# A hybrid encoder layer on one core: rows normed before the split, ten tile pairs by seven quarter products, linear attention in one written order

## The chip, the core and the metric

The kernel runs on one core of a Trainium2 chip. [...] Work moves between engines through semaphores. The metric is the time of one execution on the device in microseconds (us). The kernel of before takes 1973.33 us, the median of three runs (1972.96 to 1973.87).

## What is computed

One layer of a streaming encoder on two request groups, 1024 prompt tokens and 32 sample tokens, side by side as T = 1056 columns. D = 1024 features lie as 8 row tiles of 128 partitions.

```
h = rms(x);  z = h @ w_in  -> q,k,v,r,gate-rank | band q,k,v | gates gA,gB
A: linear attention, 4 heads: S = exp(b_last) S + (k exp(b_last - b))^T v,
   o = scores v + (q exp(b)) S,   b = cumsum(log sigmoid(...)) / 16,
   scores with a decay for each channel;  rms per head, * silu(r)
B: softmax attention over the own and the 8 last 64-token chunks, 8 heads
x += rms((sigmoid(gA) * (A @ w_a) + sigmoid(gB) * (B @ w_b)) @ w_out)
x += rms(conv feed-forward);   x += rms(sigmoid(rms(x) @ w_g) * (p @ w_ple))
```

The input product has 52 output tiles of 128 columns of w_in: 4 q, 4 k, 8 v, 8 r, 12 of the band, 8 gA and 8 gB, and a narrow one of 16 columns for the gate rank.

## The kernel before

All large products are split in two halves to keep float32 accuracy: a tensor x becomes xh (rounded to the matmul format) and xl = x - xh, a weight becomes whi and wlo, and one product takes three matmuls: whi.xh, whi.xl, wlo.xh (`product`, L224 to L230). The columns are cut into three chunks of 352 (`CHUNKS`). A tile of the input product is 8 row tiles x 3 matmuls x 3 chunks = 72 matmuls.

Up to L373 stands the start. The side input p is multiplied with w_ple first (L302 to L312), while the eight rows of x arrive. The rows are split with the norm's gain but without the norm itself (L320, L321); their squares are added on ACT, POOL and DVE (L324 to L330), and the norm's inverse root is made afterwards (L342). It is applied when a tile leaves PSUM: `to_tile` (L352) multiplies by `rstd` on DVE. `project(n, evac)` loads a weight tile (`weights`, L198; ACT makes the high half in L207, DVE or POOL the low one in L208), does its 72 matmuls and evicts each chunk.

Band attention (from L386) goes over four head pairs. Each projects q, k and v (`band_project`), splits them and turns v, and then does nine pieces of work for each of the two heads (`band_head`: scores, exponentials, transposes, product with v). After each pair `gates(n)` projects some of the 16 gate tiles, takes their sigmoid (L547) and stores them in DRAM (`BAND_GATES` = 1, 1, 1, 0).

The linear attention goes over four heads (last loop before `xp.release()`): `gla_project` makes q, k, v and turns v (L644); `gla_rest` makes r and its silu (L654); `gla_head` makes the decay b (matmul L674, Exp and Ln L677 and L678, nine scans L681), and then goes through four segments of 256 tokens (the last with 32 sample tokens more). A segment has for each of six levels a difference (L698), two exponentials (L699, L700) and two factors (L701, L702); then for each 128-token block seven small products (L730, L731), eight masked copies into `scores` (L733, L736), the output (L744, L746), a transposed key (L750), and the state's update (L755, L760). The output's norm and the product with silu(r) end it (L770 to L779). `gates` projects 2, 3, 2 and 6 gate tiles after the heads (`GLA_GATES`), and `weight_sum` lets POOL issue sums of weight blocks that the down product uses far later.

Branch B's product (L812 to L833) loads the band's results and their softmax sums (`d_ob`, `d_inv`), multiplies and splits them into `bh` and `bl`, which lie where xh lay; branch A's product, the output product, the feed-forward's up and down products and the last gate follow.

What sets the order: up to the branch products nothing is written out. The framework's scheduler gives each engine a list by program order as priority, and moves ready work ahead of work that must wait. `tc.high_priority()` raises weight splits and evictions. From the output product on, `tc.manual_schedule` keeps PE, DVE and ACT in program order. There the up product is already computed by block sums and seven quarter products in place of eight (L1188 to L1279). SP and POOL issue their transfers in their own order. Large row buffers come from the pool `ev`, tag "ev", with `EVB` = 5 buffers: each `evt()` takes the next one and waits until its last reader is done. PSUM has 3 banks of tag "mm" for projections, 3 of "one" and one double bank "two" (`PS_BAND`).

Of the kernel before, what the change touches and what calls it, by code (L numbers as in the profile page):

```python
# [11 lines left out]
F32 = mybir.dt.float32  # L12
# [35 lines left out]
EVB = 5  # L48
# [6 lines left out]
GLA_GATES = (2, 3, 2, 6)  # L55
# [33 lines left out]
ORD0 = 'rvvqk'  # L89
# [23 lines left out]
def emit(tc, a):  # L113
# [18 lines left out]
    banks = list(PS_BAND)  # L132
# [142 lines left out]

    d_pl = tl(dram, [8, P, T], tag="d_pl")
    xp = pool("xp", side="right")
    pp = pool("pp", side="right")
    ph = tl(pp, [P, 2, T], F32R, tag="ph")
    pl = tl(pp, [P, 2, T], F32R, tag="pl")  # L280
    pin = [tl(pp, [P, T], tag="pin", bufs=2) for kt in range(2)]
    for i in range(WARM):
        pe.matmul(ps_mm()[:, :P], onesM, onesM, start=True, stop=True)
    for kt in range(2):
        ac.dma_start(pin[kt][:, chunk(0)], a["p"][kt, :, chunk(0)])
    wple = [weights(a["w_ple"][0], ve, 4)]
    for c in range(NC):
        s = chunk(c)
        for kt in range(2):
            if c:  # L290
                dma.dma_start(pin[kt][:, s], a["p"][kt, :, s])
            split_hi_lo(ph[:, kt, s], pl[:, kt, s], pin[kt][:, s])
    dma.dma_start(vec, a["vec"])
    st = pool("st", side="right")
    xin = [tl(st, [P, T], tag="xin", bufs=XB) for kt in range(KT)]
    for kt in range(KT):
        if kt == XFIRST:
            wple.append(weights(a["w_ple"][1]))
        dma.dma_start(xin[kt], a["x"][kt])
    dma.dma_start(convst, a["state_conv"])  # L300
    for n in range(KT):
        hi, lo = wple[n // 4]  # L302
        z = evt()
        for c in range(NC):
            s = chunk(c)
            ps = ps_mm()[:, : s.stop - s.start]
            product(ps, hi, lo, [(2 * (n % 4) + k, k) for k in range(2)], lambda k: ph[:, k, s], lambda k: pl[:, k, s])
            if c in PLE_DVE:
                ve.tensor_copy(z[:, s], ps)
            else:  # L310
                ac.activation(z[:, s], ps, AF.Copy)
        dma.dma_start(d_pl[n], z)  # L312


    xh = tl(xp, [P, KT, T], F32R, tag="xh")
    xl = tl(xp, [P, KT, T], F32R, tag="xl")
    accx = tl(st, [P, T], tag="accx")
    for kt in range(KT):
        x = xin[kt]
        ac.activation(xh[:, kt], x, AF.Copy, scale=col(G_PRE_MIX + kt))  # L320
        ve.scalar_tensor_tensor(xl[:, kt], x, col(G_PRE_MIX + kt), xh[:, kt], op0=ALU.mult, op1=ALU.subtract)  # L321
        q = accx if kt == 0 else x
        if kt % 2:
            po.tensor_tensor(q, x, x, op=ALU.mult)  # L324
        else:
            ac.activation(q, x, AF.Square)
        if kt == 1:
            ve.scalar_tensor_tensor(accx, x, 8 * EPS, accx, op0=ALU.add, op1=ALU.add)
        elif kt > 1:
            ve.tensor_tensor(accx, accx, x, op=ALU.add)  # L330
    import contextlib
    def hpri(f):
        return tc.high_priority() if f else contextlib.nullcontext()

    log_exp()
    for c in range(NC):
        s = chunk(c)
        inv_rms(rstd(s), accx[:, s], "D", st, split=NS_START)
    st.release()
    pp.release()  # L340

# [9 lines left out]
    def to_tile(t):  # L351
        return lambda ps, s: ve.tensor_tensor(t[:, s], ps, rstd(s), op=ALU.mult)  # L352


    ap = pool("ap")
    d_alr = tl(dram, [80, T], F32R, tag="d_alr")
    alr = evt()[:16]
    war = tl(ap, [P, KT, 16], tag="war")
    dma.dma_start(war, a["w_alr"])
    was = tl(ap, [P, KT, 48], F32R, tag="was")  # L360
    ve.tensor_copy(was[:, :, 0:16], war)
    ve.tensor_copy(was[:, :, 16:32], war)
    ve.tensor_tensor(was[:, :, 32:48], war, was[:, :, 0:16], op=ALU.subtract)
    for c in range(NC):
        s = chunk(c)
        ps = ps_mm()[:48, : s.stop - s.start]
        for kt in range(KT):
            pe.matmul(ps, was[:, kt], xh[:, kt, s], start=(kt == 0), stop=False)
            pe.matmul(ps, was[:, kt], xl[:, kt, s], start=False, stop=(kt == KT - 1))
        ac.activation(alr[:, s], ps[32:48], AF.Copy)  # L370
        ve.tensor_tensor(alr[:, s], ps[0:16], alr[:, s], op=ALU.add)
        ve.tensor_tensor(alr[:, s], alr[:, s], rstd(s, 16), op=ALU.mult)
    ast = tl(ev, [P, T], F32R, tag="ev", bufs=EVB)[:80]  # L373
    po.memset(ast.bitcast(F32), 0.0)
    ac.activation(ast[0:16], alr, AF.Copy)
    ve.tensor_tensor(ast[32:48], alr, ast[0:16], op=ALU.subtract)
    ac.activation(ast[64:80], alr, AF.Copy)
    po.dma_start(d_alr, ast)

    ap.release()  # L380
# [5 lines left out]
    def band_project(hp):  # L386
# [4 lines left out]
        project(QB0 + hp, lambda ps, s: ve.scalar_tensor_tensor(qf[:, s], ps, 0.125, rstd(s), op0=ALU.mult, op1=ALU.mult))  # L391
        project(KB0 + hp, to_tile(kf))
        project(VB0 + hp, to_tile(vf))
# [145 lines left out]
    d_ga = tl(dram, [8, P, T], tag="d_ga")  # L539
    d_gb = tl(dram, [8, P, T], tag="d_gb")  # L540
    todo_gates = [(n, w, d) for n in range(8) for w, d in ((GA0, d_ga), (GB0, d_gb))]

    def gates(cnt):
        for n, w0, dst in todo_gates[:cnt]:
            g = evt()
            project(w0 + n, to_tile(g))
            ac.activation(g, g, AF.Sigmoid)  # L547
            dma.dma_start(dst[n], g)
        del todo_gates[:cnt]

    d_inv = tl(dram, [4, 2, 9 * P], tag="d_inv")
    for hp in range(4):
# [29 lines left out]
        gates(BAND_GATES[hp])  # L582
# [6 lines left out]
    d_sr = tl(dram, [8, P, T], tag="d_sr")  # L589
    gp = pool("gp")  # L590
    wa2 = None

    masks, eye, scores, scores_s = None, None, [], None


    def constants():
        nonlocal masks, eye, scores_s
        masks = tl(gp, [P, 7, 64], U8, tag="masks")
        mf = tl(gp, [P, 64], tag="mf", bufs=2)
        for l in range(7):  # L600
            m = 1 << l
            mf = tl(gp, [P, 64], tag="mf", bufs=2)
            po.memset(mf, 1.0)
            v = mf.rearrange("p (n m) -> p n m", m=m)
            pat = [[-2 * m, 64 // m], [0, m]]
            po.affine_select(out=v, in_=v, pattern=pat, compare_op=ALU.is_ge, fill=0.0, base=0, channel_multiplier=1)
            pat = [[2 * m, 64 // m], [0, m]]
            po.affine_select(out=v, in_=v, pattern=pat, compare_op=ALU.is_ge, fill=0.0, base=m - 1, channel_multiplier=-1)
            ve.tensor_copy(masks[:, l], mf)
        eye = tl(gp, [P, P], U8, tag="eye")  # L610
        ve.tensor_copy(eye, ident)
        for i in range(2):
            scores.append(tl(gp, [P, P], tag=f"scores{i}"))
            po.memset(scores[i], 0.0)
        scores_s = tl(gp, [NS, NS], tag="scores_s")
        po.memset(scores_s, 0.0)
# [1372 lines left out]
```

## Time and profile before

| | us |
|---|---|
| median of three runs | 1973.33 |
| profiled execution, span from first to last instruction | 1970.8 |
| from the first product of x's tiles (gate rank) to the first product of branch B | 39.72 to 904.11 |
| PE busy | 1924.6 |
| DVE busy | 1251.5 |
| ACT busy | 951.2 |
| POOL busy | 405.4 |

The program has one core, and PE's granted clock is 0.994 of full speed on average. A line of the groups view gives: the line of the kernel, engine and operation, the tile written and the tiles read, the shape, the count; then busy time in us, the mean of one in ns; then the engine's idle time just before these instructions and what ended it. A line of the timeline begins with the start and the duration in us. A line of the windows view gives a stretch and its length, for each engine the busy us and the number of instructions, then PE's clock, the share of the 16 DMA engines in use and GB/s. A line of the transfers view gives the destination and source, queue, count, size and the median time from issue to landing.

### The profile page before, as it was taken

How to read it: one execution, taken by the hardware profiler on the slowest of the kernel's cores; microseconds unless marked ns; L12 is line 12 of the kernel's file. 1: busy time of each engine (PE TensorE's matmuls, PEld its weight loads, DVE VectorE, ACT ScalarE, POOL GpSimd, SP SyncE). 2: the span in 40 equal slices, each digit the busy share in tenths (PEclk: the TensorE clock that was granted, in tenths of full speed). 3: DMA queues.
4: the chain of work that ended last, by engine and by line, in shares of the span. 5: the costliest groups of instructions: out<-in, count | busy, mean ns of one | idle time of the engine just before them, and what ended most of it. 6: DMA issues, size and time to landing. Idle time of an engine off the chain costs nothing.

```text
span 1970.8 us, 34508 instructions
## 1 busy us (share of the span) xinstructions
PE 1924.6 (98%) x13594; PEld 1886.2 (96%) x13594; DVE 1251.5 (64%) x2546; ACT 951.2 (48%) x1747; POOL 405.4 (21%) x470
## 2 busy tenths in 40 slices
PE   8999999999999999998999999999999999999996
PEld 7999999999999999998999989999999999999996
DVE  7556556457366475466554576787777766557776
ACT  6456455455364463564323454443333344555545
POOL 4322322143112131121120111111121211000112
PEclk9999999999999999999999999999999999999998
DMA  7212121166226253227744345644345459887755
GB/s 283 69 57 75 59 70 57 51 185 180 82 89 172 81 155 88 97 77 240 267 163 133 103 136 194 213 137 137 109 121 114 113 141 310 276 290 233 246 158 105
DMA packets 107005, 289.04 MB, mean 147 GB/s; under 512 B 11668, under 2 KB 34012, under 8 KB 106204
## 3 DMA queue, kind: packets, MB, share of 16 engines
q1 hardware_dynamic: 78924, 198.45, 31.1%
q0 software_dynamic: 27632, 88.04, 16.5%
q8 instruction: 106, 1.74, 0.4%
q14 instruction: 55, 0.45, 0.1%
q10 hardware_dynamic: 288, 0.36, 0.1%
HBM read 198.49 MB, written 111.39 MB: 157 GB/s over the span
## 4 chain that ended last, share of the span: by engine, by line
PE 80%; DVE 10%; ACT 4%; DMA 3%; issue 2%; SPq 0%; DVEq 0%; ACTq 0%
PE mm L228 13%; PE mm L229 13%; PE mm L230 13%; PE two L1212 6%; PE two L1214 6%; PE two L1213 6%; PE two L1665 3%; PE two L1664 3%; PE two L1663 3%; PE one L508 2%; PE two L730 2%; PE one L466 1%; DVE d L698 1%; PE two L450 1%; PE one L744 1%
## 5 line engine op out<-in xcount | busy, mean ns | idle before, releaser
L228 PE MATMUL mm<-xh,whi 128*128 128x352 f32 x1248 | 412.1, 330 | 0.0
L230 PE MATMUL mm<-xh,wlo 128*128 128x352 f32 x1248 | 411.9, 330 | 0.0
L229 PE MATMUL mm<-xl,whi 128*128 128x352 f32 x1248 | 409.7, 328 | 0.0
L208 POOL TENSOR_TENSOR wlo<-raw,whi 128x512 fp32r<-128x512 f32 x130 | 183.8, 1422 | 680.6 <-ACT whi L207 628.1
L228 PEld LDWEIGHTS mm<-xh,whi 128*128 128x128 f32 x1248 | 235.3, 189 | 1.6 <-DVE ev L352 0.4
L229 PEld LDWEIGHTS mm<-xl,whi 128*128 128x128 f32 x1248 | 235.0, 188 | 1.7 <-issue 0.3
L230 PEld LDWEIGHTS mm<-xh,wlo 128*128 128x128 f32 x1248 | 234.6, 188 | 1.1
L1665 PE MATMUL two<-d,wlo 128*128 128x264 f32 x616 | 175.5, 285 | 1.2 <-DVE wlo L1407 1.2
L1664 PE MATMUL two<-d,whi 128*128 128x264 f32 x616 | 174.7, 284 | 2.0 <-DVE d L1358 2.0
L1663 PE MATMUL two<-d,whi 128*128 128x264 f32 x616 | 174.7, 284 | 0.4 <-ACT d L1357 0.4
L207 ACT ACTIVATE whi<-raw 128x512 fp32r<-128x512 f32 (+1 forms) x146 | 89.4, 621 | 156.8 <-PE mm L229 95.3
L1214 PE MATMUL two<-mh,wlo 128*128 128x264 f32 x576 | 163.0, 284 | 0.0
L1213 PE MATMUL two<-ml,whi 128*128 128x264 f32 x576 | 162.9, 284 | 0.0
L1212 PE MATMUL two<-mh,whi 128*128 128x264 f32 x576 | 161.2, 284 | 0.0
L1664 PEld LDWEIGHTS two<-d,whi 128*128 128x128 f32 x616 | 115.8, 188 | 2.4 <-DVE d L1358 2.4
L1665 PEld LDWEIGHTS two<-d,wlo 128*128 128x128 f32 x616 | 115.6, 188 | 1.6 <-DVE wlo L1407 1.6
L1663 PEld LDWEIGHTS two<-d,whi 128*128 128x128 f32 x616 | 116.4, 189 | 0.6 <-ACT d L1357 0.6
L1214 PEld LDWEIGHTS two<-mh,wlo 128*128 128x128 f32 x576 | 108.4, 188 | 0.0
L1213 PEld LDWEIGHTS two<-ml,whi 128*128 128x128 f32 x576 | 108.4, 188 | 0.0
L1212 PEld LDWEIGHTS two<-mh,whi 128*128 128x128 f32 x576 | 107.3, 188 | 0.0
L352 DVE TENSOR_TENSOR ev<-mm,rstd 128x352 f32<-128x352 f32 x120 | 61.4, 518 | 54.5 <-PE mm L230 53.9
L1202 ACT ACTIVATE whi<-ws 128x512 fp32r<-128x512 f32 x72 | 45.4, 631 | 102.0 <-PE two L1213 76.7
(534 smaller groups left out, 5178.6 us busy)
## 6 DMA issues: line engine op xcount, KB each, us to landing
raw<-in_w_in SPq DMA_DIRECT2D x52, 512.0 KB, 4.0
uraw<-d_b SPq DMA_DIRECT2D x34, 528.0 KB, 5.7
d_b<-av POOLq DMA_DIRECT2D x33, 528.0 KB, 3.5
d_ws<-in_w_down POOLq DMA_DIRECT2D x24, 704.0 KB, 12.1
raw<-in_w_up SPq DMA_DIRECT2D x27, 512.0 KB, 3.7
wraw<-d_ws SPq DMA_DIRECT2D x16, 704.0 KB, 6.0
d_b<-gc POOLq DMA_DIRECT2D x11, 792.0 KB, 5.7
sraw<-in_w_up SPq DMA_DIRECT2D x17, 512.0 KB, 4.6
```

The costliest lines, as they stand in the source:

```text
L207: ac.activation(hi[-1][:, d], raw[:, b], AF.Copy)
L208: eng.tensor_tensor(lo[-1][:, d], raw[:, b], hi[-1][:, d], op=ALU.subtract)
L228: pe.matmul(ps, h, xh(kt), start=(first and i == 0), stop=False)
L229: pe.matmul(ps, h, xl(kt), start=False, stop=False)
L230: pe.matmul(ps, l, xh(kt), start=False, stop=(last and i == n - 1))
L352: return lambda ps, s: ve.tensor_tensor(t[:, s], ps, rstd(s), op=ALU.mult)
L1212: pe.matmul(ps[:, j, :HC], w[0][:, k], x[0][:, k, s], start=st, stop=False, skip_group_check=True)
L1213: pe.matmul(ps[:, j, :HC], w[0][:, k], x[1][:, k, s], start=False, stop=False, skip_group_check=True)
L1214: pe.matmul(ps[:, j, :HC], w[1][:, k], x[0][:, k, s], start=False, stop=sp_, skip_group_check=True)
L1663: pe.matmul(o, wh, xh_[:, s], start=(k == 0 and p in (0, 4, 5)), stop=False, skip_group_check=True)
L1664: pe.matmul(o, wh, xl_[:, s], start=False, stop=False, skip_group_check=True)
L1665: pe.matmul(o, wl, xh_[:, s], start=False, stop=(k == HD - 1 and p in (3, 4, 6)), skip_group_check=True)
```

## The change

1. The start (up to the first tile pairs) is written out in one fixed order for PE, DVE and ACT. x is loaded by column halves; each half's norm is made between the products of p, the rows are multiplied with gain and norm, and only then split. Evictions no longer multiply by the norm, and most go to ACT. The band's first q, k and v tiles and the gate rank are computed by halves of 528 columns (two matmuls of 264) and stored; the band loads them back. Beside the second half, DVE makes the block sums of x for the next step.

2. The eight r tiles, the eight gB tiles and the first four gA tiles are computed as ten pairs by `in_strassen`: two weight tiles and x form a 2 x 2 block product, done with seven quarter products of 4 row tiles x 2 x 264 columns x 3 matmuls = 168 matmuls a pair. This stage comes before band attention. The order in it is the scheduler's.

3. Between band pair 2 and 3 the tiles k and q of head 0 are projected and stored. No gate tile is left in the band's stage.

4. The linear attention is in one written order over 16 segments. Decay differences, exponentials and factors are made for the segment after the one whose products run; masked copies and state updates take two blocks at once; the root and result of a segment come in the next one. Three projection chunks ("units") stand in each segment: 12 tiles of heads 1 to 3 and the last four gA tiles, whose sigmoid is moved to branch A's product.

5. `EVB` goes from 5 to 4.

```diff
-EVB = 5
+EVB = 4
-GLA_GATES = (2, 3, 2, 6)
+GLA_GATES = (0, 0, 1, 3)
+GA_DENSE = 4
...
+    def x_norm(h, i):
+        for k in range(2 * i, 2 * i + 2):
+            ve.scalar_tensor_tensor(xrow(k)[:, h], xrow(k)[:, h], col(G_PRE_MIX + k), ys[h.start], op0=ALU.mult, op1=ALU.mult)
+        ac.activation(xh[:, 2 * i : 2 * i + 2, h], xrow(2 * i, 2)[:, :, h], AF.Copy)
+
+    def x_low(h, i):
+        b = slice(2 * i, 2 * i + 2)
+        ve.tensor_tensor(xl[:, b, h], xrow(2 * i, 2)[:, :, h], xh[:, b, h], op=ALU.subtract)
...
+    S = {0: [lambda: p_split(1)], 1: [lambda: p_split(2)], 2: [lambda: first_load(0)],
+         4: [lambda: x_square(one, 0)], 5: [lambda: x_square(one, 1)],
+         6: [lambda: x_add(one, 1)], 7: [lambda: x_square(one, 2), lambda: wple.append(next(raw_split(raws[1], eng=po))), lambda: first_load(1)], 8: [lambda: x_add(one, 2)],
+         9: [lambda: x_square(one, 3)], 10: [lambda: x_add(one, 3), lambda: x_sums(one)],
+         12: [lambda: x_inverse(one)], 13: [lambda: x_norm(one, 0)], 14: [alr_weights, lambda: first_split(2), lambda: first_load(2)],
...
+    plain_half(0, one, first_hook)
+    plain_half(1, one, second_hook)
+    plain_half(2, one)
+    alr_half(one)
...
+    plain_half(0, two, sum_hook(0))
+    plain_half(1, two, sum_hook(1))
+    plain_half(2, two, sum_hook(2))
+    alr_half(two)
...
+        def mul(ps, w, n, first, last):
+            x = XIN[n]
+            for j in range(2):
+                s = slice(j * HC, (j + 1) * HC)
+                for k in range(HK):
+                    st, sp_ = first and k == 0, last and k == HK - 1
+                    pe.matmul(ps[:, j, :HC], w[0][:, k], x[0](k, s), start=st, stop=False, skip_group_check=True)
+                    pe.matmul(ps[:, j, :HC], w[0][:, k], x[1](k, s), start=False, stop=False, skip_group_check=True)
+                    pe.matmul(ps[:, j, :HC], w[1][:, k], x[0](k, s), start=False, stop=sp_, skip_group_check=True)
...
+    for n in range(0, 8, 2):
+        in_strassen(R0 + n, R0 + n + 1, AF.Silu, d_sr[n], d_sr[n + 1])
+    for w0, d, top in ((GB0, d_gb, 8), (GA0, d_ga, GA_DENSE)):
+        for n in range(0, top, 2):
+            in_strassen(w0 + n, w0 + n + 1, AF.Sigmoid, d[n], d[n + 1])
...
+    def to_tile(t, eng=0, scale=1.0):
+        if eng:
+            return lambda ps, s: ve.tensor_copy(t[:, s], ps)
+        return lambda ps, s: ac.activation(t[:, s], ps, AF.Copy, scale=scale)
...
+    for u in range(16):
...
+        if u < 15:
+            differences(u + 1)
+        level_products(u)
+        key_turns(u)
+        loads(u)
+        if u:
+            roots(u - 1)
+            later()
+            results(u - 1)
+        if u < 15:
+            exponentials(u + 1, range(1, 5))
+        key_copies(u)
+        score_copies(u)
+        if u < 15:
+            factors(u + 1, range(1, 5))
+            exponentials(u + 1, range(5, 8))
+        first = unit()
+        split_tile()
+        load_tile()
...
+        updates(u)
+        first()
+        if u < 15:
+            factors(u + 1, range(5, 8))
...
+        second = unit()
+        next(chain, None)
...
+        outputs(u)
+        second()
+        squares_a(u)
+        later = unit()
...
+        for i in range(2):
+            next(chain, None)
+        sums_a(u)
...
+        if n >= GA_DENSE:
+            ac.activation(g, g, AF.Sigmoid)
```

More of the change, by code (lines that the diff above doesn't have):

```diff
@@ L315, in emit @@
[L315 to L330, printed above, removed]
```

880 lines of the change are left out of this document (635 added, 245 removed).

## The prediction

> **What bounds the kernel now.** I read the page's busy times and chain first:
>
> ```profile
> span 1970.8 us, 34508 instructions
> PE 1924.6 (98%) x13594; PEld 1886.2 (96%) x13594; DVE 1251.5 (64%) x2546; ACT 951.2 (48%) x1747; POOL 405.4 (21%) x470
> ...
> PE 80%; DVE 10%; ACT 4%; DMA 3%; issue 2%; SPq 0%; DVEq 0%; ACTq 0%
> ```
>
> TensorE (PE) is busy in 98% of the span and makes 80% of the chain, so a change is worth what it takes off PE's work plus what it does to PE's gaps. Busy time can't price a matmul, because matmuls overlap (a row's duration is over twice the spacing). So I took the timeline of two dense stretches, whose first column is the start, and divided.
>
> ```profile
> 59.73 0.32 PE L230 MATMUL mm<-xh,wlo 128*128 128x352 f32 x1
> ...
> 62.98 0.32 PE L229 MATMUL mm<-xl,whi 128*128 128x352 f32 x1
> ```
> ```profile
> 1339.78 0.29 PE L1214 MATMUL two<-mh,wlo 128*128 128x264 f32 x1
> ...
> 1342.95 0.28 PE L1214 MATMUL two<-mh,wlo 128*128 128x264 f32 x1
> ```
>
> The first stretch has 21 matmuls of 352 columns, 20 steps in 3.25 us: 0.1625 us each. The second, in the up product, which is already computed by seven quarter products, has 27 of 264 columns: 26 steps in 3.17 us, 0.1219 us each. Both are 0.462 ns a column.
>
> Then I looked for PE's gaps with windows (per engine: busy us and instructions; then PE's clock, DMA share, GB/s) and the DVE groups of the start:
>
> ```profile
> 25.00:30.00 5.00, 2.86 (x17) 2.28 (x16) 5.00 (x6) 3.36 (x7) 2.13 (x2) 1.00 0.91 369
> 30.00:35.00 5.00, 3.11 (x18) 2.53 (x16) 5.00 (x4) 2.44 (x4) 5.00 (x3) 1.00 0.47 172
> 35.00:40.00 5.00, 3.96 (x13) 3.80 (x14) 5.00 (x6) 1.36 (x2) 1.67 (x1) 0.50 0.39 160
> ```
> ```profile
> L321 DVE SCALAR_TENSOR_TENSOR xl<-xin,vec,xh 128x1056 fp32r<-128x1056 f32 x8 | 13.8, 1728 | 2.4 <-ACT xh L320 2.3
> ```
> ```profile
> 4.86 0.42 PE L228 MATMUL mm<-ph,whi 128*128 128x352 f32 x1 [0.22 <-ACT ph L233]
> ...
> 48.54 1.77 PE one L253 x6
> ```
>
> The start is loose: its first product begins at 4.86 us; from 25 to 40 us PE gets 17, 18 and 13 matmuls into 5 us, where full speed holds 31, DVE is full, and the clock falls to 0.50. The last matmuls of the start, those of the input's mean square, run from 48.54 to 50.31 us; dense products of the input begin there. DVE's row split (L321) takes 1728 ns on average. The next loose place is the end of the linear attention:
>
> ```profile
> 890.00:900.00 10.00, 10.00 (x68) 10.00 (x67) 8.32 (x26) 6.26 (x14) 1.65 (x2) 1.00 0.89 256
> 900.00:910.00 10.00, 7.83 (x39) 6.62 (x36) 9.17 (x22) 6.35 (x13) 1.15 (x1) 0.83 0.75 218
> 910.00:920.00 10.00, 7.11 (x38) 5.18 (x38) 5.19 (x16) 2.83 (x8) 0.00 (x0) 0.95 1.02 335
> ```
>
> From 900 to 920 us stand 77 matmuls, where the 10 us before hold 68: 59 are missing, at 10/68 us each 8.7 us.
>
> **The ten tile pairs.** Before, a pair of output tiles took 2 x 3 chunks x 8 x 3 = 144 matmuls of 352 columns, 23.40 us. Now it takes 7 products x 24 = 168 of 264, 20.48 us. That is 2.92 us a pair and **29.2 us** for ten, and it can't be hidden, as PE is the bound. The new stage must feed PE from DVE: per pair 4 block sums, 7 low halves and 5 evictions. The up product shows all three and that PE stays full beside them:
>
> ```profile
> 1300.00:1400.00 100.00, 100.00 (x823) 100.00 (x823) 76.19 (x125) 39.04 (x56) 15.49 (x34) 1.00 0.40 135
> ```
> ```profile
> L1203 DVE TENSOR_TENSOR wlo<-ws,whi 128x512 fp32r<-128x512 f32 x68 | 46.6, 685 | 0.4 <-ACT whi L1202 0.3
> L1195 DVE TENSOR_TENSOR ws<-raw,ws 128x512 f32<-128x512 f32 x18 | 12.4, 691 | 0.5
> L1269 DVE TENSOR_TENSOR c<-p,two 128x528 f32<-128x528 f32 x17 | 11.9, 700 | 0.9 <-PE two L1214 0.9
> ```
>
> 4 x 0.69 + 7 x 0.685 + 5 x 0.70 = 11.1 us of DVE in 20.5 us. Transfers are 1.0 MB of weights and 1.1 MB of results in 20.5 us, about 100 GB/s, where the up product ran under 135. The order here is the scheduler's own, so I take 2 us of loss over the ten pairs (0 to 10).
>
> [...]
>
> **The start.** Before, three tiles more (3 x 72 x 0.1625 = 35.1 us) would bring the kernel to 85.4 us, where the first pair of the new kernel stands. Now: first product at 5.4 us instead of 4.86 (one table load more ahead of it, 1283 ns as in the L256 row below, partly under the transfers); 144 matmuls of 352 columns, 23.4 us; the mean square of the first half, whose matmuls stand between groups 10 and 11 of these products, so that all later groups queue behind them while PE waits for DVE's additions (about 2 us); then 6 half tiles and the two gate-rank halves, 288 and 64 matmuls of 264, 42.9 us. DVE's work during the first product is 26 us and ACT's 28 us by my count of the hooks (eight row norms of 528 columns at 0.70 as in the L1269 row above, four low halves and three additions of 1056 at 1.4, eight evictions, ten splits), so PE can't finish at 28.8; I take 35 us (31 to 42). The POOL squares beside L321, which took 1.73 us where L1269's rate gives 1.4, are gone. During the second half's norm DVE has 18 us in PE's 21 us, and then 20 us of block differences in 21 us: covered, but only just (a loss of up to 5). 35 + 43 + 1 = 79 against 85.4: **-6 us** (-12 to +5).
>
> **Band attention.** The same work in this stage, over fewer filler tiles. One head pair of before, with three projections and one gate tile:
>
> ```profile
> 171.48:246.59 75.11, 73.23 (x496) 69.95 (x494) 44.88 (x100) 41.76 (x97) 22.14 (x18) 1.00 0.21 66
> ```
>
> PE holds 73 of 75 us; without the gate tile it has 61 us against DVE's 45 and ACT's 42, so PE remains the bound. Projections write PSUM before their buffer is free, three chunks deep, so four "ev" buffers instead of five cost little: +2 us (0 to 12). Head pair 0's q, k, v and head 0's q, k now go through DRAM, ten issues more on SP's queue of 0.53 MB each; SP has no work of its own, and they lie under the last pair and the last head pair.
>
> **Into the linear attention.** Before, six projection tiles of head 0 (70 us) lay over its decay chain. Two are left. The chain waits for the last band attention, whose buffers its tiles take: three decay matmuls and their evictions 2, Exp and Ln 1.1 each (L678 below), nine scans 3.9 (L681 below), the odd-token factor 2.6, differences 3.1, then exponentials and factors that trail by about 5: 19 us, an estimate from the rows below. Value transposes cover 2 us and what is left of the two value tiles about 5, the rest of them being used up as filler of the last head pair. **+12 us** (0 to 19).
>
> **The linear attention in fixed order.** Small matmuls of one 128-token block, and of the state update:
>
> ```profile
> 883.72 0.38 PE L744 MATMUL one<-scores,vt 128*128 128x128 f32 x2
> ...
> 886.20 0.41 PE L228 MATMUL mm<-xh,whi 128*128 128x352 f32 x1
> ```
> ```profile
> 880.05 0.43 PE one L755 x2
> ```
>
> One block's from 883.72 to 886.20: 2.48 us. A segment has two blocks, two updates at 0.43, about 1.7 us of diagonals, sums and value turns, and three units of 24 x 0.1625: 4.96 + 0.86 + 1.7 + 11.7 = 19.2 us of PE. DVE's groups of before:
>
> ```profile
> L736 DVE COPY_PREDICATED scores<-masks,two 128x64 f32<-128x64 uint8 x203 | 50.2, 247 | 23.2 <-PE two L731 18.7
> L698 DVE TENSOR_TENSOR d<-b 128x256 f32<-128x256 f32 x80 | 33.9, 442 | 0.0
> L777 DVE SCALAR_TENSOR_TENSOR ot<-ot,vec,rs 128x256 f32<-128x256 f32 x22 | 13.2, 643 | 0.2
> L760 DVE SCALAR_TENSOR_TENSOR state<-state,bl,one 128x256 f32<-128x256 f32 x27 | 12.9, 478 | 9.5 <-PE one L755 9.3
> L681 DVE TENSOR_TENSOR_SCAN b<-ev,ev 128x128 f32<-128x128 f32 x32 | 11.6, 435 | 12.3 <-ACT ev L678 12.3
> L778 DVE TENSOR_TENSOR ot<-ot,sr 128x256 f32<-128x256 f32 x21 | 9.2, 469 | 0.0
> L733 DVE COPY_PREDICATED scores<-eye,one 128x128 f32<-128x128 uint8 x30 | 7.5, 299 | 10.5 <-PE one L718 10.4
> L260 DVE SCALAR_TENSOR_TENSOR rs<-y,y 128x256 f32<-128x256 f32 x11 | 7.3, 666 | 0.2
> L709 DVE TENSOR_TENSOR x<-x,qk 128x256 f32<-128x256 f32 x12 | 6.1, 507 | 0.0
> L258 DVE TENSOR_TENSOR y<-y 128x256 f32<-128x256 f32 x11 | 5.0, 456 | 19.6 <-ACT y L257 16.9 <-PE mm L230 2.7
> ```
>
> A segment ahead: six differences and the key's 3.1; six factors now over 256 columns at 0.507 and one over 512 at up to 0.94, 4.0; masks over two blocks at once, not in the trace, between the 64-column 0.247 and the 128-column 0.299 row, I take 0.30: with the diagonal 2.5; states 0.96; squares 0.9; three root steps of 0.46 to 0.67 and the result, 1.6 + 2 x 0.64 + 0.94 = 3.8; a quarter of the head's decays 1.8. Sum 17.0 of 19.2 us. ACT:
>
> ```profile
> L207 ACT ACTIVATE whi<-raw 128x512 fp32r<-128x512 f32 x66 | 40.7, 626 | 86.6 <-PE mm L229 45.4 <-issue 41.2
> L699 ACT ACTIVATE d<-d 128x128 f32<-128x128 f32 x80 | 24.4, 305 | 20.0 <-DVE d L698 19.2 <-DVE x L702 0.3
> L256 ACT ACT_TABLE_LOAD x14 | 18.0, 1283 | 0.3
> L678 ACT ACTIVATE ev<-ev 128x1056 f32<-128x1056 f32 x4 | 4.3, 1086 | 0.0
> ```
>
> 12 x 0.305 + 2 x 0.626 for one weight tile + three evictions of 0.5 and some 5 more = 11.4 us; the table loads (14 on L256 alone) go, worth nothing because ACT has slack. In the fixed order DVE waits twice a segment (for the roots, for the outputs), by my walk through the order 1 to 2 us in all, which just fits. I take 0 against before's order (-5 to +45, the upper end at 22 us a segment). POOL keeps one weight tile's split a segment, and the sums of the down weights are queued on it at each head's start as before.
>
> **Out of it.** The last projection unit ends the reading of the split x, and the branch B tiles take its place. Their loads:
>
> ```profile
> d_ga<-ev SPq DMA_DIRECT2D x8, 528.0 KB, 3.0
> ev<-d_inv SPq DMA_DIRECT2D x8, 264.0 KB, 7.1
> ```
>
> Two "ev" buffers a head pair: the first pair and half of the second are loaded ahead; then the last gate tile is evicted (1.5 us by my estimate), stored (3.0), a 7.1 us load follows, and the last pair waits for buffers once more: 22 us after the last unit, of which PE has 27 early products, 4.4 us. 17 us against 8.7 before: **+8 us** (-5 to +15). Branch A's four sigmoids on ACT (1.1 us each) lie beside 11.7 us of products: nothing.
>
> **Sum.** -29.2 + 2 - 6.4 + 2 + 12 + 0 + 8 = -11.6 us. The profiled execution spans 1970.8 us, the runs' median is 1973.3, so 2.5 lie outside the span: 1961.7, **1962 us**, its own range 1946 to 1972.
>
> Half clock adds little: at 35 to 40 us the row above has 0.50 after a loose stretch, 2.5 us lost in 5. Two longer gaps could cost that each, inside their ranges. [...]
>
> **Rivals.** (A) All is covered: the hand-overs cost nothing, since the scheduler keeps tiles back for them; 1962 - 12 - 8 - 4 = 1938. For it: the band row above keeps PE at 73 of 75 us through such a hand-over. Against it: fillers are counted above, and there are few. Chance 0.2. (B) The fixed order turns the linear attention into DVE's: at 17.0 us of work in 19.2, each wait that the order puts in DVE's path counts. It decides from 0.73 us a segment (11.6 / 16) beyond 19.2; at 21 us a segment the time is 1962 + 16 x 1.8 = 1991, slower. For it: L736 and L258 wait 23.2 and 19.6 us for PE and ACT in the rows above. Against: PE had 2.2 us to give. Chance 0.2. (C) The hand-overs lie open whole: 19 into, 25 out of the linear attention and 8 more between head pairs: 1962 + 7 + 8 + 8 = 1985. Chance 0.15. (D) The quarter products gain nothing, because each pair loses 2.9 us at its start: 1962 + 27 = 1989; the up product speaks against it. Chance 0.05. The forecast has 0.4.
>
> Range 1934 to 1992: A's value with 4 us of its start, B's and C's whole. A measurement can tell about 0.2%, 4 us. Faster: A and 0.37 of the forecast, 0.57. Same: the forecast's edge (0.03) and the milder half of C, 0.11. Slower: B, the rest of C, D: 0.32.
>
> **What would show it.** The first pair's product begins near 79 us, and ten pairs take about 207 us; a pair shows 168 matmuls 0.122 us apart. Between the last band matmul and the first level product PE has about 12 us without work, and after the last projection unit about 17. Segments of the linear attention repeat every 19 to 20 us, with DVE near 17 busy. The forecast is wrong if segments take over 20 us, if a pair takes over 21.5, or if the hand-overs hold no gap.

## The result and the profile after

The changed kernel takes 2007.12 us, the median of four runs (2004.17 to 2009.63), against 1973.14 for the kernel before in the same series: 1.0177 times as long, 95% interval 1.0162 to 1.0193. It is slower by 34 us where 1962 was forecast. The profiled execution spans 2005.9 us for 1970.8.

The page of the kernel after, its span, busy times and chain (PE is TensorE, DVE VectorE, ACT ScalarE, POOL GpSimd and SP SyncE):

```profile
span 2005.9 us, 34950 instructions
PE 1923.8 (96%) x13924; PEld 1885.6 (94%) x13924; DVE 1290.3 (64%) x2333; ACT 923.9 (46%) x1790; POOL 335.0 (17%) x422
...
PE 83%; DVE 6%; DMA 4%; ACT 3%; issue 3%; POOL 1%; SPq 0%; ACTq 0%; DVEq 0%; POOLq 0%
```

PE's busy time is almost the same (1923.8 us for 1924.6), though the pairs take 29 us of work off it, and the span is 35 us longer: the time lies in gaps and in lost clock, which makes busy time longer (a 352-column matmul took 0.32 us at 752 us, where the clock was 1.00, and 0.49 at 763 us, where it was 0.50). The windows of both kernels, cut at the same events, show where. The events are the first product of p, the end of the start (before: of the band's first three tiles; after: the start of the first pair), the last matmul of each band head pair, the first level product of the linear attention, the last input projection (with which the linear attention ends in the kernel after), and the first product of branch A. The kernel before:

```profile
4.86:85.40 80.54, 74.07 (x417) 67.49 (x418) 55.59 (x70) 42.31 (x68) 37.87 (x27) 0.96 0.54 194
85.40:169.14 83.74, 83.67 (x565) 81.30 (x563) 45.32 (x100) 42.14 (x93) 21.92 (x17) 1.00 0.19 60
169.14:244.43 75.29, 73.41 (x497) 70.13 (x496) 45.00 (x102) 41.93 (x96) 22.13 (x18) 1.00 0.21 67
244.43:320.33 75.90, 75.28 (x508) 72.13 (x507) 44.57 (x102) 42.03 (x96) 22.22 (x18) 1.00 0.20 63
320.33:392.99 72.66, 72.41 (x491) 69.59 (x490) 33.90 (x90) 40.41 (x93) 11.06 (x11) 1.00 0.18 57
392.99:432.70 39.71, 39.71 (x253) 39.38 (x252) 17.96 (x44) 17.36 (x34) 21.30 (x40) 1.00 0.77 202
432.70:898.90 466.20, 458.34 (x3033) 448.11 (x3033) 284.22 (x867) 245.62 (x509) 103.55 (x89) 1.00 0.40 117
898.90:971.20 72.30, 67.24 (x408) 62.61 (x407) 42.62 (x106) 27.00 (x47) 11.47 (x9) 0.95 0.69 230
```

The kernel after, with the ten tile pairs as its second row:

```profile
5.00:89.42 84.42, 73.38 (x504) 70.45 (x504) 67.07 (x83) 46.28 (x75) 13.13 (x8) 0.96 0.47 170
89.42:294.33 204.91, 204.90 (x1681) 204.51 (x1681) 106.28 (x159) 80.67 (x115) 4.61 (x4) 1.00 0.35 110
294.33:389.95 95.62, 81.39 (x513) 76.47 (x511) 55.56 (x102) 48.87 (x106) 32.43 (x27) 0.91 0.25 85
389.95:465.12 75.17, 67.33 (x436) 63.87 (x435) 40.41 (x91) 39.05 (x97) 18.95 (x16) 0.93 0.14 46
465.12:538.58 73.46, 71.91 (x472) 69.19 (x471) 36.88 (x81) 41.71 (x103) 18.94 (x16) 0.96 0.21 68
538.58:590.31 51.73, 46.42 (x323) 42.25 (x322) 31.33 (x87) 31.11 (x83) 9.24 (x17) 1.00 0.15 46
590.31:615.00 24.69, 19.48 (x105) 17.99 (x104) 16.05 (x48) 14.97 (x44) 11.81 (x24) 0.86 0.81 232
615.00:944.00 329.00, 326.00 (x2178) 316.00 (x2178) 227.64 (x564) 148.16 (x423) 60.49 (x60) 0.97 0.48 127
944.00:1006.10 62.10, 53.19 (x292) 50.22 (x291) 26.84 (x50) 14.47 (x26) 10.47 (x9) 0.89 0.73 236
```

I call "open" the length less PE's busy time, plus the length times what the clock column lacks to 1.00. (The expectations below count the same gaps as length less matmuls times spacing, which gives 42.8 us for the band where these rows give 45.7.)

| stage | forecast of the step | before | after | difference |
|---|---|---|---|---|
| start, to the first pair | -6.4 | ends at 85.4 | ends at 89.4 | +4.0 |
| ten pairs against twenty tiles | -29.2 + 2 | 10 x 23.40 = 234.0 | 204.9 | -29.1 |
| band head pairs, open | +2 | 2.8 | 45.7 | +42.9 |
| into linear attention, open | +12 | 0 | 8.7 | +8.7 |
| linear attention, open | 0 | 7.9 | 12.9 | +5.0 |
| out of it, to branch A, open | +8 | 8.7 | 15.7 | +7.0 |
| sum | -11.6 | | | +38.5 |

The last column accounts for the 35.1 us between the spans within 3.4; the clock column has two digits, which is worth up to 1.6 us in the 329 us row.

The pairs gave what was forecast: 1681 matmuls in 204.91 us, 0.1219 us each. The band took it all away and more. The second head pair shows it in the plainest way: it lasts 75.17 us after and 75.29 before, although it has 61 matmuls less in it (436 for 497; a gate tile has 72). Its length didn't follow PE's work; the tile had been running in the holes between splits, scores, exponentials and transposes. I call such work of other tiles, which PE can do while a stage waits for its own chain, "cover".

The largest hole is at the start of head pair 0. Windows of the kernel after:

```profile
300.00:310.00 10.00, 7.49 (x49) 7.03 (x47) 9.88 (x5) 6.45 (x14) 9.23 (x9) 1.00 0.55 213
310.00:320.00 10.00, 3.39 (x9) 2.34 (x10) 7.95 (x18) 2.01 (x7) 2.31 (x2) 0.56 0.33 105
320.00:330.00 10.00, 9.64 (x60) 8.78 (x60) 4.11 (x10) 5.96 (x16) 0.00 (x0) 0.92 0.00 0
```

One of PE's waits in the band stage, in us, times and the longest:

```profile
PE two L750 <- DVE kl L735: 6.0, 1, 6.0
```

VectorE in that hole, from the timeline (start, duration):

```profile
299.76 6.17 DVE L730 TENSOR_TENSOR kl<-ev,kh 64x1056 fp32r<-64x1056 f32 x2 [4.53 <-ACT kh L729]
305.96 3.77 DVE L730 TENSOR_TENSOR kl<-kc,kh 64x512 fp32r<-64x512 f32 x2
...
312.63 1.98 DVE L735 CAST kl<-kl 64x1568 fp32r<-64x1568 f32 x2
```

From 310 to 320 us PE has 9 matmuls. It waits 6.0 us in one piece for the last copy of the low key part (kl); that copy begins at 312.63, behind the subtractions and the cached values' split, which fill DVE from 299.76 on. The only other PE work, the next pair's q projection, fills its three PSUM buffers by 307 us and stops, because its evictions stand on ACT behind exponentials that wait for the same chain (they run from 323.05 us on). The clock of that stretch is 0.56.

### The profile page after: what moved, and what is told of

Read it like the earlier page. It is cut to its first block, busy times and chain, and to the rows that moved or that the text cites. A ratio compares the mean times of both kernels' runs of the same rounds, so it can differ in the third digit from the quotient of the medians.

```text
span 2005.9 us, 34950 instructions
## 1 busy us (share of the span) xinstructions
PE 1923.8 (96%) x13924; PEld 1885.6 (94%) x13924; DVE 1290.3 (64%) x2333; ACT 923.9 (46%) x1790; POOL 335.0 (17%) x422
## 4 chain that ended last, share of the span: by engine, by line
PE 83%; DVE 6%; DMA 4%; ACT 3%; issue 3%; POOL 1%; SPq 0%; ACTq 0%; DVEq 0%; POOLq 0%
PE mm L229 11%; PE mm L231 10%; PE mm L230 10%; PE two L1729 6%; PE two L1731 6%; PE two L1730 6%; PE two L614 3%; PE two L616 3%; PE two L615 3%; PE two L2176 3%; PE two L2175 3%; PE two L2174 3%; PE two L1067 2%; PE one L807 2%; PE one L765 1%
## 5 line engine op out<-in xcount | busy, mean ns | idle before, releaser
L229 PE MATMUL mm<-xh,whi 128*128 128x352 f32 x696 | 236.9, 340 | 0.9 <-ACT ev L934 0.7
L231 PE MATMUL mm<-xh,wlo 128*128 128x352 f32 x696 | 229.3, 329 | 0.0
L230 PE MATMUL mm<-xl,whi 128*128 128x352 f32 x696 | 228.5, 328 | 0.0
L209 POOL TENSOR_TENSOR wlo<-raw,whi 128x512 fp32r<-128x512 f32 x50 | 67.6, 1355 | 426.9 <-ACT whi L208 422.6
L229 PEld LDWEIGHTS mm<-xh,whi 128*128 128x128 f32 x696 | 133.7, 192 | 3.7 <-issue 1.3
L230 PEld LDWEIGHTS mm<-xl,whi 128*128 128x128 f32 x696 | 133.5, 192 | 0.4
L231 PEld LDWEIGHTS mm<-xh,wlo 128*128 128x128 f32 x696 | 132.8, 191 | 0.3
L330 POOL TENSOR_TENSOR wlo<-raw,whi 128x512 fp32r<-128x512 f32 x38 | 51.7, 1378 | 259.3 <-ACT whi L329 259.3
L614 PE MATMUL two<-th,whi 128*128 128x264 f32 x320 | 91.0, 284 | 0.0
```

The source lines that it names most:

```text
L209: eng.tensor_tensor(lo[-1][:, d], raw[:, b], hi[-1][:, d], op=ALU.subtract)
L229: pe.matmul(ps, h, xh(kt), start=(first and i == 0), stop=False)
L230: pe.matmul(ps, h, xl(kt), start=False, stop=False)
L231: pe.matmul(ps, l, xh(kt), start=False, stop=(last and i == n - 1))
L614: pe.matmul(ps[:, j, :HC], w[0][:, k], x[0](k, s), start=st, stop=False, skip_group_check=True)
```

## The experiments

Times are medians, ratios are to the kernel before measured beside it, with the 95% interval. The kernel before had medians of 1971.6 to 1972.6 us there. Edits are to the changed kernel unless said otherwise.

**1. Linear attention without the written order.** The same instructions, left to the framework's scheduler.

```diff
-    gla = tc.manual_schedule(engines={mybir.EngineType.PE, mybir.EngineType.DVE, mybir.EngineType.Activation})
-    gla.__enter__()
...
-    gla.__exit__(None, None, None)
```

> The changed kernel with the written order of the linear attention taken out: the same instructions, ordered by the scheduler as in the rest of that half. Theory O (the order costs: segments repeat every 20.6 us where their PE work was put at 19.2): the segments come back to about 19.3 us and the time falls by about 20 us, to 1987. Theory C (cover: the loss lies in the band attention and its two hand-overs, where too few projection tiles are left to fill PE): no more than 5 us either way, 2002 to 2012, unless the scheduler now moves tiles of heads 1 to 3 back into the hand-over before the linear attention, which could save up to 15. Theory B (four ev buffers instead of five hold projections up): 2002 to 2012.

1989.84 us, ratio 1.0097 (1.0077 to 1.0116): 17.3 us back, half of the loss. Windows of linear attention and of the way to branch A, cut at the last input projection as above (here at 919.9 us; the last product of linear attention comes at 933.9):

```profile
617.64:919.90 302.26, 302.26 (x2125) 296.08 (x2124) 205.16 (x540) 142.29 (x411) 61.34 (x60) 1.00 0.49 134
919.90:987.60 67.70, 58.73 (x317) 54.76 (x317) 30.97 (x68) 15.97 (x30) 10.47 (x8) 0.90 0.73 227
```

From the end of the last head pair to branch A it takes 395.6 us (592.0 to 987.6) instead of 415.8 (590.3 to 1006.1). Up to the last input projection PE has no gap and the full clock: linear attention is open 0 us for 12.9, of which 9.9 were clock. The way out is as open as with the written order, 15.7 us. Ahead of the first level product stand 133 matmuls for 105, and 6.5 us are open there for 8.7. The first head pair of the band stays as it was:

```profile
296.20:391.85 95.65, 81.39 (x514) 76.73 (x512) 55.59 (x102) 48.87 (x106) 32.40 (x27) 0.91 0.25 85
```

So the written order costs 17 us, most of it inside the linear attention and there mostly as clock, and it is not what opened the band.

**2. The band's output in a buffer of its own.** A way to test whether the four row buffers hold the next projection up.

```diff
-        ob = evt()
+        ob = tl(bp, [P, T], tag="ob")
```

> The changed kernel with the band's result tile ob in a buffer of its own, so that q, k and v of the next head pair and the fills have four ev buffers among them, as with five before. Theory B (buffers): the holes of 10 us and more at the starts of head pairs 1, 2 and 3 shrink, 15 to 25 us faster, 1982 to 1992. Theory C (cover): the fill tiles are only moved, 2000 to 2010. Theory O (order): 2002 to 2012.

2001.08 us, 1.0149 (1.0131 to 1.0167). Windows of its four head pairs:

```profile
295.20:394.90 99.70, 94.57 (x610) 91.12 (x609) 57.41 (x102) 51.86 (x114) 36.53 (x29) 0.97 0.27 89
394.90:477.20 82.30, 82.06 (x556) 79.49 (x556) 44.42 (x91) 43.44 (x106) 23.52 (x19) 1.00 0.20 64
477.20:545.80 68.60, 59.34 (x365) 54.81 (x364) 42.80 (x93) 36.93 (x91) 18.51 (x16) 0.87 0.18 55
545.80:584.40 38.60, 33.22 (x214) 28.20 (x213) 27.32 (x76) 28.12 (x79) 3.74 (x12) 0.88 0.07 24
```

The first two pairs are nearly closed (open 8.1 and 0.2 us), the last two open up (18.2 and 10.0). The sum is 36.5 us for 45.7, and the time lies in the 2000 to 2010 us of theory C. A free buffer lets later projections run earlier, and then they are missing later: the stage has too little other work, wherever it is put.

**3. Cover put back.** The four gA tiles that had become two pairs are plain tiles again, one behind each head pair; the other four stay in linear attention.

```diff
-GA_DENSE = 4
+GA_DENSE = 0
...
-    todo_gates = list(range(GA_DENSE, 8))
+    todo_gates = list(range(4))
...
         dma.dma_start(d_ob[hp], ob)
+        gates(1)
...
-[gate_tile(n) for n in range(GA_DENSE, 8)]
+[gate_tile(n) for n in range(4, 8)]
```

> The changed kernel with the last two pairs of seven quarter products undone: gA tiles 0 to 3 are plain projections again, one after each head pair of the band, as gate tiles stood before. PE's work grows by 2 x 2.9 = 5.8 us. Theory C (cover): 46.8 us of tiles fill the holes of the band stage (61 us lost there); I expect half of it to be won, 2007 + 6 - 25 = 1988 (1978 to 1998). Theory B (buffers): a gate tile takes one more ev buffer, 2013 or more. Theory O: 2013.

1991.06 us, 1.0098 (1.0072 to 1.0123): 16.1 us back, though the kernel has 5.8 us more of matmuls. Windows of its head pairs:

```profile
254.40:351.20 96.80, 86.94 (x560) 82.65 (x559) 56.76 (x104) 49.34 (x106) 33.50 (x27) 0.93 0.28 89
351.20:426.90 75.70, 75.38 (x508) 72.20 (x507) 41.40 (x95) 41.05 (x99) 21.87 (x18) 1.00 0.22 67
426.90:498.60 71.70, 71.63 (x486) 68.75 (x485) 32.13 (x83) 40.91 (x101) 15.52 (x16) 1.00 0.23 74
```

Two pairs less in the dense stage save 40.8 us there (204.9 to 164.1); four tiles more in the band cost 23.2 (296.0 to 319.2). The second head pair again lasts 75.7 us, now with the tile in it; the first lasts 96.8 for 95.6 and the third 71.7 for 73.5. The first keeps 16.6 us open. My reading is that all four row buffers are taken there, so that a gate tile has nowhere to go; run 7 tests it.

**4. The kernel before with four row buffers.**

```diff
-EVB = 5
+EVB = 4
```

> The kernel of before with four ev buffers instead of five and nothing else changed. Theory B (buffers): the band and the branch B stage lose 10 us or more, 1983 or more. Theory C and O: tiles enough to fill PE are there, so at most 4 us, 1973 to 1977.

1978.96 us, 1.0036 (1.0022 to 1.0051): 7 us, none of them in the band. Its first head pair, and the way from linear attention to branch A:

```profile
85.00:167.60 82.60, 82.51 (x557) 80.11 (x556) 44.76 (x99) 40.94 (x90) 21.78 (x17) 1.00 0.19 61
897.30:977.10 79.80, 69.92 (x408) 64.20 (x407) 43.37 (x108) 25.97 (x46) 11.31 (x9) 0.91 0.66 209
```

The 7 us lie between the marks of the theories (10 or more, at most 4). The way out is open 17.1 us for 8.7 with five buffers. The fifth buffer mattered where results are loaded back, and in a band that has cover it doesn't matter.

**5. Experiments 1 and 3 together.**

> Linear attention left to the planner and four plain gate tiles behind the band head pairs, both at once. The two edits gave 17.3 and 16.1 us alone, from 2007.1 us. If the holes of the band and those of the linear attention are separate losses, they add: 1974 us (1969 to 1979), about the time before the change. If one hole had only moved from the one stage to the other, the second edit gives little: 1985 us or more.

1973.86 us, 1.0004 (0.9994 to 1.0013). Cover and written order are separate losses (17.3 and 16.1 us alone, 33.3 together), and together they are the whole distance to the time before. The eight pairs that are left take 23.4 us off PE's work all the same: that gain is still spent, for instance in the first head pair, open 14.5 us here, and ahead of the linear attention, 8.1.

**6. The start reordered.** The split of the second w_ple tile stands behind the last square of the first half, the sums one product later, the split of the key weights first in its hook.

```diff
-7: [lambda: x_square(one, 2), lambda: wple.append(next(raw_split(raws[1], eng=po))), lambda: first_load(1)],
+7: [lambda: x_square(one, 2), lambda: first_load(1)],
-9: [lambda: x_square(one, 3)], 10: [lambda: x_add(one, 3), lambda: x_sums(one)],
+9: [lambda: x_square(one, 3), lambda: wple.append(next(raw_split(raws[1], eng=po)))],
+10: [lambda: x_add(one, 3)], 11: [lambda: x_sums(one)],
...
-            wfirst[n] = next(raw_split(raws[n], eng=po))
+            wfirst[n] = next(raw_split(raws[n], eng=ve if n == 3 else po))
...
+            first_split(3)
             x_square(two, 3)
             x_add(two, 1)
-            first_split(3)
```

> Only the start is reordered: the second weight tile of the first projection is split after the last square of the first half of the rows, the sums go one product later, and the split of the key weights comes first in its hook with its low part on VectorE. Theory (the sums of squares stand on ScalarE behind a split that waits for its own transfer): the gap of 15 to 21 us shrinks to 2 or 3 us, the half clock behind it goes, and the first tile pair starts 6 to 9 us earlier: 2000 us (1997 to 2003). Rival (the first projection is held by the arrival of the rows themselves): the gap stays, within 2 us of 2007.

2009.26 us, 1.0190 (1.0175 to 1.0205): nothing gained. The kernel after had its gap at 15 us:

```profile
15.00:20.00 5.00, 1.55 (x10) 1.26 (x8) 1.83 (x2) 3.18 (x6) 2.50 (x2) 1.00 1.04 396
45.00:50.00 5.00, 2.09 (x12) 1.67 (x11) 4.19 (x4) 3.62 (x6) 3.21 (x2) 0.84 0.23 89
```

The reordered one:

```profile
15.00:20.00 5.00, 3.40 (x21) 3.01 (x19) 3.78 (x4) 2.61 (x6) 3.31 (x2) 1.00 1.05 395
45.00:50.00 5.00, 0.00 (x0) 0.00 (x0) 4.83 (x3) 2.23 (x4) 2.65 (x1) 0.95 0.24 84
```

The first gap closed (10 matmuls became 21), as the theory said, but the time didn't fall: a whole gap opened at 45 us, where the sums of the second half wait in PE's order for DVE. The first pair starts at 89.1 us for 89.4.

**7. Four edits together:** 1, 2, 3 and 6.

> Four edits together: planner's order in linear attention, four plain gate tiles behind the band head pairs, the band's output in a buffer of its own, the reordered start. If the losses are separate, 2007.1 - 17.3 - 16.1 - 6.0 - 7 = 1961 us (1956 to 1968), faster than the kernel before the change. If they cover one another, 1970 us or more.

1963.24 us, 0.9955 (0.9940 to 0.9969), faster than the kernel before. Its four head pairs:

```profile
254.50:359.30 104.80, 103.44 (x685) 100.48 (x684) 60.28 (x107) 52.62 (x114) 38.40 (x31) 1.00 0.27 91
...
523.50:563.40 39.90, 34.30 (x242) 29.61 (x242) 27.80 (x78) 29.27 (x81) 6.24 (x14) 0.99 0.11 36
```

With cover and a free buffer both, three head pairs are closed (open 1.4 us, 0.2 and 0.3) and the last is open 6.0 us. The buffer alone had left the last two open, cover alone the first.

**8. The high key half's copy from GpSimd to ScalarE.**

```diff
-KHC = 2
+KHC = 1
```

> The copy of the high key half is moved from GpSimd to ScalarE; nothing else. Theory C (the band lacks other TensorE work): VectorE's low key part gets shorter than its 3.4 to 6.2 us, but the holes stay within 8 us of their 42.8, 2000 to 2010 us. Rival P (the holes come from VectorE running beside GpSimd): the low key part falls to about 1.5 us and the band loses 20 us less: 1985 to 1992 us.

2000.95 us, 1.0146 (1.0131 to 1.0161). The band is open 37.2 us for 45.7. The time falls by 6 us, just inside the 2000 to 2010 us of theory C and far from P. VectorE's part of the first hole:

```profile
300.49 6.17 DVE L730 TENSOR_TENSOR kl<-ev,kh 64x1056 fp32r<-64x1056 f32 x2 [4.53 <-ACT kh L729]
306.69 1.40 DVE L730 TENSOR_TENSOR kl<-kc,kh 64x512 fp32r<-64x512 f32 x2
```

The two subtractions of the cached keys fell from 3.77 to 1.40 us, the first two kept their 6.17 (in the kernel after GpSimd's two subtractions for qs, 2.48 and 2.69 us, lie beside them). The copy's place on GpSimd accounts for 6 us of the loss, not for the hole as such.

**9. As 6, and the second sums issued later** (`x_sums(two)` at k = 6 for k = 1, the inverse at k = 7 for 4).

> The reordered start of the run before, and the sums of squares of the second half of the rows issued five inner steps later (k = 6 for 1), so that TensorE does not stand at 45 to 50 us behind VectorE's sums. Theory (each of TensorE's own waits costs; the second sums had taken over the gap of the first): the first tile pair starts at 84 to 86 us for 89.1, 2003 us (2000 to 2006). Rival (VectorE, 4.2 of each 5 us busy from 25 us on, sets the end of the start whatever TensorE does): the first pair stays at 88 us or later, 2006 to 2010 us.

2008.31 us, 1.0181 (1.0166 to 1.0197). The gap moved again:

```profile
45.00:50.00 5.00, 4.53 (x37) 4.32 (x36) 4.83 (x4) 2.59 (x4) 2.04 (x1) 1.00 0.39 111
60.00:70.00 10.00, 7.74 (x63) 7.45 (x62) 9.66 (x13) 4.76 (x10) 0.00 (x0) 1.00 0.01 2
```

PE is now busy 4.53 us of the 5 from 45 us on and loses 2.3 us from 60 to 70, where DVE is busy 9.66 of 10. The first pair starts at 88.0, and the time is within the rival's marks. PE's gaps change their place and hardly the end of the start.

**10. The edits of 7, 8 and 9 together.**

> All edits that gained, together: planner's order in linear attention, four plain gate tiles behind the head pairs, the band's output in its own buffer, the start as in the run beside it, the key copy on ScalarE. From 1963.2 us: the key copy gave 6 alone, but in that kernel the band loses only 11.9 us, most of it in the last head pair, so 1 to 3 us are left for it; the start gives 0 or 4. 1959 us (1954 to 1963).

1965.52 us, 0.9966 (0.9953 to 0.9979), where 1959 was expected: no better than run 7. With cover in the band, the key copy and the later sums add nothing that can be told. Its linear attention up to the last input projection, and the way from there to branch A:

```profile
586.70:899.70 313.00, 309.81 (x2136) 302.66 (x2135) 215.14 (x553) 143.49 (x412) 61.92 (x60) 0.98 0.48 131
899.70:964.95 65.25, 55.55 (x314) 52.64 (x314) 27.64 (x54) 15.24 (x29) 10.31 (x9) 0.90 0.73 230
```

**11. As 10, with a fifth gate tile moved from linear attention behind the last head pair.**

```diff
-        gates(1)
+        gates(1 if hp < 3 else 2)
```

> As the run beside it, with a fifth gate tile moved from linear attention behind the last head pair, where 8.8 us were open and 6.5 in the hand-over after it. If TensorE work is what the last head pair lacks, the open time there falls by 8 us or so; whether linear attention then opens decides the sum: 1953 us if it has cover to spare, 1959 if the gap only moves there.

1950.85 us, 0.9891 (0.9874 to 0.9907): the fastest of all, 22 us below the kernel before. Its last head pair and the same two windows:

```profile
517.00:569.80 52.80, 49.61 (x343) 46.18 (x342) 29.90 (x81) 30.67 (x83) 9.21 (x17) 0.99 0.16 50
...
598.40:883.10 284.70, 284.70 (x1975) 279.17 (x1975) 195.45 (x513) 135.14 (x396) 55.54 (x55) 0.99 0.49 134
883.10:951.10 68.00, 64.10 (x398) 60.94 (x397) 38.22 (x93) 19.27 (x39) 11.24 (x9) 0.95 0.73 235
```

Run 11 is run 10 with one tile moved, and 14.7 us below it. The last head pair is still open 3.7 us. The way from the last input projection to branch A is open 7.3 us for 16.2 in run 10, and the linear attention up to that projection 2.8 for 9.5; so most of the gain over run 10 came at another place than the expectation named. The last input projection ends 39 us before the linear attention does, where run 10 had 7. My reading is that branch B's loads, which take the place of the split x, begin that much earlier against the end of the attention; no run tests this alone.

The gain over run 7 is not explained by it. Run 7 is open about 10 us in these two stretches taken together, as run 11 is, and the medians lie 12.4 us apart, but the profiled executions only 4.8 (1960.60, the fastest of the one kernel, and 1955.84, the slowest of the other).

**12. As 11, with two of the four low parts of the sums given to GpSimd.**

```diff
-        ve.tensor_tensor(ts[i][1][:, :, k], xr[i][:, :, k], ts[i][0][:, :, k], op=ALU.subtract)
+        (po if k else ve).tensor_tensor(ts[i][1][:, :, k], xr[i][:, :, k], ts[i][0][:, :, k], op=ALU.subtract)
```

> As the fastest run so far (1950.9 us), with two of the four low parts of the sums for the quarter products (2.35 us each on VectorE) given to GpSimd. Theory (VectorE's own work sets the end of the start): the first tile pair starts at 84 to 86 us for 87.8, 1948 us (1945 to 1951). Rival P (GpSimd beside VectorE slows it: the sum of two halves took 2.7 us beside GpSimd and 0.7 without): the first pair stays at 87 us or later, 1951 us or more.

1960.89 us, 0.9955 (0.9938 to 0.9971): 10 us slower than run 11, the first pair at 87.6 for 87.8: rival P. The profiled executions lie only 1.7 us apart (1957.51 and 1955.84, the fastest of the one kernel and the slowest of the other); they show the pairs 4.3 us longer (168.4 for 164.1), and not where the rest of the medians' difference lies. GpSimd's timeline:

```profile
73.26 4.77 POOL L539 TENSOR_TENSOR tl<-xr,th 128x2112 fp32r<-128x2112 f32 x1 [24.38 <-ACT th L536]
```

and VectorE's:

```profile
73.36 5.79 DVE L528 TENSOR_TENSOR xr<-xr 128x1056 f32<-128x1056 f32 x1
```

The block difference that takes 1.25 us elsewhere took 5.79: it ended 1.1 us after GpSimd's instruction had ended at 78.0. Of the 4.7 us that GpSimd took off DVE, 4.5 came back in this one instruction.

## Why the prediction was wrong

**The step that failed is the band's cover.** The prediction compared busy sums: without the gate tile, 61 us of PE against 45 of DVE and 42 of ACT, "so PE remains the bound", and priced the stage at +2 us. It measured +42.9. PE was full before only because other tiles filled the holes of each head pair; with little cover a head pair's length is set by its own chain, in which the engines wait for one another, and not by the busiest of them. Experiment 3 shows it: with the tile back, the second head pair keeps its length (75.7 us). Experiment 2 shows that a buffer alone mostly moves the holes, 7 that cover and buffer together close all but the last. Even the upper end of the step, 12 us, was less than a third of what it cost. Rival C had the right place, head pairs whose hand-overs lie open, but gave them 8 us.

**Ten pairs: right.** 204.9 us for 204.8, with no loss at all where 2 us were allowed.

**The start: wrong by 10 us.** It ends 4.0 us later than before, inside the stated -12 to +5, where -6.4 was taken. The prediction saw that DVE was "covered, but only just" and then added up PE's work. Runs 6 and 9 show that PE's gaps don't decide: they were moved twice, and the first pair came at 89.1 and 88.0 us. What speaks for VectorE is the wait of the first pair in the kernel after, 1.26 us for an eviction on DVE (L494), which stands behind unbroken DVE work from 71 us on. Run 12 didn't settle it: it took work off DVE, most of which came back as waiting, and the first pair stood at 87.6.

**Into and out of linear attention: right in kind, smaller in size.** +8.7 for +12, +7.0 for +8. The reason given for the way out, loads that wait for row buffers, is borne out by run 4, where one buffer less opens it by 8.4 us, and by run 1, which has four buffers without the written order and is as open there as with it (15.7 us).

**The written order: price too low.** 0 was taken. Segments repeat every 20.4 us, from the first level products of the first and of the last segment (15 segments apart; the 20.6 of the first expectation counts to a later product of the last one):

```profile
614.96 0.85 PE L1067 MATMUL two<-x 128*128 128x64 f32 x3
...
921.64 0.66 PE L1067 MATMUL two<-x 128*128 128x64 f32 x4
```

That is over the 20 us named as the mark of an error, but rival B's reason was wrong as well: DVE is busy 227.64 us in 329, 14.2 a segment for the 17.0 counted, and not the bound. PE is busy 326.0 of 329.0; 3 us are gaps and about 10 are clock. Without these 12.9 us a segment would be 19.6 us by my estimate, near the 19.2 counted for PE. Run 1 puts the cost of the order at 17 us. Without it the same stage has no gap and no lost clock up to its last input projection, so what the prediction put at nothing is mostly this clock, which busy sums don't show. The table's +5.0 is less because the kernel before was itself open 7.9 us there.

**The sum.** The span was forecast to fall by 11.6 us and rose by 35.1, a miss of 46.7. The band makes 40.9 of it, the start 10.4, the written order 5.0; into, out and the pairs came better than forecast by 3.3, 1.0 and 1.9; the 3.4 that the table leaves over are the rest. No rival had the band as its place alone.

## What to carry to other kernels

Busy sums for each engine don't say what a stage lasts: look at whether its length changes between two of its repetitions that hold different amounts of filler work. Here the second head pair lasted 75 us with the tile and without it, so the tile was nearly free there, and making it 12% cheaper in a stage of its own made it cost its whole price. Before work is moved out of a stage, leave in it as much as its chain leaves open, with a free buffer for its result. And read the clock column of a stage in written order: here PE was recorded as busy for 326 of 329 us and lost some 10 us to the clock, which the scheduler's order of the same instructions did not.

## What the hardware showed that was not expected

**A VectorE instruction beside GpSimd took 4.5 us longer.** 1.25 us became 5.79 in run 12, with an end 1.1 us after that of GpSimd's instruction of 4.77 us, and the two subtractions of the cached keys take 3.77 us in the kernel after and 1.40 in run 8, where one copy has left GpSimd. Not every instruction grew: the two evictions of L494 took 0.76 us beside GpSimd's second subtraction in run 12 (from 85.42 us on, 4.72 us long) and 0.75 in the kernel after, which has no such subtraction. What makes the difference, no run shows.

**The clock fell while PE was recorded as busy throughout.** Windows of the kernel after, in linear attention:

```profile
740.00:755.00 15.00, 15.00 (x99) 14.81 (x98) 11.98 (x33) 6.03 (x17) 2.52 (x2) 1.00 0.25 74
755.00:765.00 10.00, 10.00 (x56) 9.33 (x56) 7.76 (x25) 5.51 (x21) 0.47 (x1) 0.67 0.18 52
```

From 755 to 765 us PE has no idle time in the records and none in the 15 us before, but the clock is 0.67, with 56 matmuls in 10 us where the 15 before hold 99. A busy time with modelled ends may hide short gaps between small matmuls, which no run here decides. The stage has two more falls of this kind (0.59 from 843 to 847 us and 0.66 from 925 to 930), and all three begin 4 to 5 us into a row of small products; a fourth, 0.51 from 612 to 622, begins in the hand-over ahead of the stage, behind gaps of 1.5 and 1.1 us. Inside the stage they are some 10 us of clock together. In run 1, which has the same products in the scheduler's order, the clock is 1.00 from the first level product to 919.9 us. What sets the falls off stays open.
